# A third Strassen pair in the second w_o_b group, with memory statistics, value forms and one join moved

## The chip, the core and the metric

The kernel runs on one core of one Trainium2 chip. The metric is the device time of one launch in microseconds (us). The core's engines work side by side, each through its own list of instructions in order: PE (matrix products; PEld is its loading of the stationary operand), DVE (elementwise vector work), ACT (elementwise scalar work and copies), POOL, and SP, which here issues nearly all transfers. They wait for one another through semaphores.

## The reference

One layer of a streaming encoder for 256 tokens of width 2048, in float32. Cut to what matters:

```python
h = LN(alpha*h + 0.5*SwiGLU_1(h))                       # ffn1: 2048 -> 2*5504 -> 2048
proj = h @ w_in                                          # q/k/v of A, latents of B, both gates
y_a = chunked_relbias_attention(...) @ w_o_a
y_b = mla_attention(...) @ w_o_b                         # w_o_b: 2048 x 2048
h = LN(alpha*h + (g_a*y_a + g_b*y_b) @ w_out)            # w_out: 2048 x 2048
m = LN(mem)                                              # 256 memory tokens
q = h @ w_xq;  k, v = split(m @ w_xkv)                   # cross-attention, 4 heads of 512
h = LN(alpha*h + softmax(q k^T) v @ w_xo)
h = LN(alpha*h + 0.5*SwiGLU_2(h))                        # ffn2
```

## The kernel before, in words

**Numbers.** Every operand of a product is split in two: `hi`, a rounded copy that ACT makes (`halves` and `split`, lines 264 and 255), and `lo`, the rest, which DVE makes by a subtraction (lines 267 and 256). A product then takes three matmuls: hi by hi, hi by lo, lo by hi.

**Weights.** A weight arrives as 1 MB pieces (`raw`, a ring of three tiles) which SP loads, in the order of use. `load` in `run` makes `hi` and `lo` of a piece some pieces ahead of its use. An item of work with a weight is called a block here.

**Pairs of groups.** `pair_group` computes 1024 output columns (two times 512) for all 256 tokens in blocks that each cover two of the 16 tiles of 128 along the contraction. A plain block (`mm_pair`, line 311) is 2 tiles x 2 token halves x 2 column halves x 3 matmuls = 24 matmuls of 512 columns. A block that stands in the tuple `AT_...` is done as a Strassen pair (`mm_sums`, line 366): seven products in place of eight, so 21 matmuls. It costs more elsewhere. The seven products need sums of weights (`weight_sums`, lines 248 and 250 on DVE, into the tile that `sums_in` names), whose hi and lo are made as well, so that 3584 columns are split in place of 2048; and they need sums of activations, the forms (`forms_step`, `sum_forms`, lines 321 and 325, and a split). `SUMS_...` says where a form is kept: `None` is four small tiles of a ring, a name and a number is half of a block of memory that stays. At the end of the pairs `shared` (lines 679 to 684) combines the four shared sums out of PSUM.

**PSUM.** There are eight banks, four called `mm` and four called `at`. A group uses four for its own sums and the other four for its pairs' shared sums; the next group takes the banks over as they come free.

**Order.** `weave(main, side)` puts side work in front of the item with the given number of a group's list: numbers 0 to 7 are mostly the blocks, and `shared` takes a number of its own behind the last pair. A planner that knows costs then orders each engine's instructions; among work that is ready, what stands earlier in the program goes first, and a `prio` (SOON is 400 instructions) moves work ahead.

**The places that the change touches.**

- `out_b(g)`, group g of 0 and 1 of `w_o_b`. In group 0 the blocks 2, 4 and 6 are pairs, in group 1 the blocks 4 and 6. When a group ends, its `done` (lines 1282 to 1284) scales and adds with the gates, copies planes, and the sides `send` (a transposing transfer on SP) and `turn` (`join`, line 854 on ACT, then a split) prepare the input of `w_out`. The sides of group 0 run inside group 1, those of group 1 inside `w_out`.
- `mem_norm`, which normalizes the memory tokens beside the blocks of `w_out`: `stat(0)` and `stat(1)` take mean and spread of each half (four `bn_stats`, line 390, a chain of small DVE operations, two products with the identity, line 1358), `spread` broadcasts them with small matmuls (line 1368), and `quarter(0..3)` applies them. `stat` is bound to come behind the last `lo` before it, `spread` behind the last matmul before it.
- `cross`, whose `val(0)` computes half of the values in eight blocks of `w_xv` with pairs at 2, 4 and 6. `form_v(2)` is made in the group before, `form_v(4)` and `form_v(6)` inside `val(0)`, into block T3.
- `ffn`, whose last group of columns has 384 columns a side in place of 512 (n = 3). The hidden activations of the group before it are joined and split (`turn` in `hidden`) inside it. Each `ffn` has one such group.

Of the kernel before, what the change touches and what calls it, by code (L numbers as in the profile page):

```python
# [30 lines left out]
            {3: ("X1", 0), 5: ("X1", 1), 7: ("X0", 0)})  # L31
SUMS_GATE, AT_GATE = {**SUMS_IN, 5: ("F", 0)}, ((2, 4, 5, 6), (2, 4, 5, 6), (2, 4, 6), (2, 4, 6))
ORDER_GATE = (0, 2, 1, 4, 5, 3, 6, 7)
SUMS_YB = {4: ("T0", 0), 6: ("T0", 1), 2: None}
AT_YB = (2, 4, 6), (4, 6)
SUMS_XQ = {4: ("H5", 0), 6: ("H5", 1), 2: None}
SUMS_XV = {4: ("T3", 0), 6: ("T3", 1), 2: None}
SUMS_XO = {2: None, 4: ("H2", 0), 6: ("H2", 1)}
# [63 lines left out]
class Kernel:  # L102
# [451 lines left out]
    def ffn(self, tag, xT, st, first=None, steps=None, late=None, before=None, tags=None):  # L554
# [4 lines left out]
        turn = None  # L559
        fx = {}  # L560
        for half, nf in enumerate(F_SPLIT):
# [3 lines left out]
            for g in range(-(-nf // 4)):  # L565
                j, n = f0 // 4 + g, min(4, nf - 4 * g)
                qs, ps = {}, {}
                if j == 2 and first is not None:
                    self.add(self.load_rest)
                if j == 0 and first is not None:  # L570
                    main, (ps, qs, fx) = [], first
                    self.add(lambda qs=qs: self.shared(qs, 512), prio=SOON)
                elif j == 0 and before:
                    main = self.collect(self.first_group, tag, xT, before, ps, fx)
                else:
                    src = t[tag + "_w_in"][j] if n == 4 else t[tag + "_w_in_r"][0]
                    main = self.collect(self.pair_group, bank, src, n * P, KT, xT, SUMS_IN, fx, ps, qs, None, SUM_HOME + ("H5",))
                if turn and n < 4:
                    turn[5] = turn.pop(6)
                self.weave(main, turn or {}, prio=0)  # L580
                for c, (home, _) in homes.items():
                    if home == "X1" and c // 2 == g - 1:
                        self.add(form(c))
                hidden, turn = self.hidden(ps, bank, g, n, hid, qs)
                self.add(hidden, prio=SOON)
                if before and 2 <= j < 6:
                    self.add(lambda q=j - 2: self.gb_apply(2, self.h, (q,)), prio=LATE)
                if j == 0 and first is not None:
                    for c in set(SUMS_IN) - set(AT_FIRST):
                        self.add(self.forms_step(fx, SUMS_IN, c, xT, False))  # L590
                bank ^= 1
# [14 lines left out]
            side = dict(turn)  # L606
# [9 lines left out]
            turn = None  # L616
# [714 lines left out]
    def mem_norm(self):  # L1331
# [12 lines left out]
        def stat(tt):  # L1344
            def fn():
                if tt == 0:
                    e["diag"] = self.w2((P, 4, P))
                    e["ones"] = self.w1((P, P))
                    nc.gpsimd.memset(e["ones"], 1.0)
                st = self.ln_begin()  # L1350
                with self.tc.issue_after(self.last_lo.ins):
                    for n in range(4):
                        self.ln_piece(st, e["m"][tt], n)
                kept = self.chain
                mean, r, _ = self.ln_scale(st)
                self.chain = kept
                for k, v in enumerate((mean, r)):
                    nc.vector.tensor_scalar(e["diag"][:, 2 * k + tt, :], self.ident, v, None, ALU.mult)
                if tt:
                    e["mT"] = self.act(["H0", "H1", "H2", "H3"])  # L1360
            return fn
# [10 lines left out]
        def quarter(q):  # L1372
            def fn():
                v = e["raw"][q // 2][:, q % 2 * 4:q % 2 * 4 + 4, :]
                for k, op in enumerate((ALU.subtract, ALU.mult)):
                    nc.vector.tensor_tensor(v, v, e["mr"][:, k].to_broadcast([P, 4, S]), op)
                for j in range(4):
                    kt = 4 * q + j
                    nc.scalar.activation(v[:, j, :], v[:, j, :], AF.Identity,
                                         bias=self.vec("mem_ln_b", kt), scale=self.vec("mem_ln_g", kt))  # L1380
                self.split(v, e["mT"].blk(0, 4 * q, 4), e["mT"].blk(1, 4 * q, 4))
            return fn

        return {0: [load], 2: [stat(0)], 6: [stat(1)], 8: [spread], 9: [quarter(0)], 11: [quarter(1)], 13: [quarter(2)], 14: [quarter(3)]}

    def turned_norm(self, ln, st, x):

# [45 lines left out]
    def cross(self, xT, st, norm, steps_out):  # L1433
# [116 lines left out]
        form_v = lambda c: self.forms_step(fv, SUMS_XV, c, m)  # L1550
# [3 lines left out]
        def group(build, side, *args):  # L1554
            got = {}
            main = self.collect(lambda: got.update(build(*args) or {}))
            self.weave(main, side, prio=0)
            return got

        def both(one, two):  # L1560
            return {i: one.get(i, []) + two.get(i, []) for i in {*one, *two}}
# [9 lines left out]
                     8: [nsend(1, 3), njoin(1, 2)]}, 0, 8)  # L1571
        side = group(query, {1: [njoin(0, 3)], 2: [njoin(1, 3), form_q(4)], 4: [form_q(6)], 6: [form_q(2)]}, 0)
        side = group(query, both(side, {4: [form_v(2)]}), 1)
        group(val, both(side, {2: [form_v(4)], 4: [form_v(6)]}), 0)
        group(keys, {0: [ready(0)], 2: [scores(0), gb(0)], 3: [send(0), ready(1)], 4: [gb(1)], 5: [join(0), scores(1)],
                     6: [out(0), ready(2), send(1), gb(2)], 8: [join(1)]}, 8, KT)
        group(val, {1: [out(1), ready(3), scores(2)], 3: [send(2), scores(3), gb(3)], 5: [join(2), send(3)],
# [199 lines left out]
```

## Time and profile before

| what | us |
|---|---|
| median of 3 runs (lowest, highest) | 2434.77 (2434.17, 2435.91) |
| the profiled execution: its time | 2432.52 |
| the profiled execution: its span | 2430.7 |
| PE busy | 2422.3 |
| DVE busy | 2130.9 |
| ACT busy | 1553.2 |
| PE idle and waiting for another engine, all waits | 4.1 |

The profiled execution took 2.25 us less than the median. Its span runs from the first to the last instruction; 1.8 us of its time lie around it. Starts and stretches are given in us from the start of the span. In a row of the timeline, the number in brackets is the idle time of the engine before the row and what ended it; a row that stands for several instructions ends with their count, and the length of a row of matmuls includes 0.16 us of the last one's drain, in which the next has begun. In a row of windows there stand the length of the stretch, the busy time of each engine with the count of the instructions that touch the stretch, the granted TensorE clock (1.00 is full), the busy share of the DMA engines and GB/s.

The stages that the change touches, by the start of their first matmul:

| stage | us |
|---|---|
| last group of ffn1 | 547.90 to 580.81 |
| w_o_b, group 0 | 1200.94 to 1242.42 |
| w_o_b, group 1 | 1242.42 to 1284.58 |
| w_out, group 0 | 1284.58 to 1329.07 |
| first half of the keys | from 1373.50 |
| values, val(0) | 1502.22 to 1545.08 |
| last group of ffn2 | 2286.50 to 2319.49 |

### The profile page before, as it was taken

The numbers are of one execution on the slowest core, as the hardware profiler recorded it, in microseconds if no ns is written. First come the engines' busy times: TensorE is split into PE (matmuls) and PEld (weight loads), VectorE is DVE, ScalarE is ACT, GpSimd is POOL, SyncE is SP. The second block draws the span as 40 slices with busy tenths as digits, with TensorE's granted clock in tenths as the row PEclk, the third lists the DMA queues.
The fourth block names the chain that finished last, engine by engine and source line by source line (L and its number), as shares of the span: only waits on it lengthen the run. The fifth ranks groups of instructions, "written<-read, shape, count | busy, mean of one in ns | idle before, by whom it ended". The sixth has DMA issues, their size and how long they took to land.

```text
span 2430.7 us, 29702 instructions
## 1 busy us (share of the span) xinstructions
PE 2422.3 (100%) x11280; PEld 2022.8 (83%) x11280; DVE 2130.9 (88%) x2437; ACT 1553.2 (64%) x2022; POOL 35.9 (1%) x81
## 2 busy tenths in 40 slices
PE   9999999999999999999999999999999999999999
PEld 8888888888888888888888888888888888888887
DVE  8999989899889998779788889979879999888997
ACT  6676745666555557878565687765666675556662
POOL 0000000000000001000000000000000000000000
PEclk9999999999999999999999999999999999999999
DMA  7766656667656657776577577655556766666665
GB/s 268 252 212 214 207 200 222 210 201 219 224 176 215 216 195 248 229 210 176 183 246 256 167 241 213 220 181 192 190 199 214 229 221 210 220 207 207 200 220 182
DMA packets 176414, 516.20 MB, mean 212 GB/s; under 512 B 111728, under 2 KB 112496, under 8 KB 121104
## 3 DMA queue, kind: packets, MB, share of 16 engines
q1 hardware_dynamic: 170816, 495.83, 61.6%
q0 software_dynamic: 4592, 17.30, 2.2%
q8 instruction: 88, 1.44, 0.2%
q10 hardware_dynamic: 864, 1.18, 0.1%
q14 instruction: 54, 0.44, 0.1%
HBM read 485.30 MB, written 2.10 MB: 201 GB/s over the span
## 4 chain that ended last, share of the span: by engine, by line
PE 89%; DVE 4%; ACT 3%; DMA 1%; issue 1%; SPq 0%; DVEq 0%; ACTq 0%
PE at L311 24%; PE mm L311 23%; PE at L366 11%; PE mm L366 11%; PE mm L298 10%; PE mm L277 4%; PE mm L279 2%; DVE lo L267 2%; ACT hi L264 1%; PE at L1034 1%; PE at L1505 0%; PE at L277 0%; DMA raw<-w_xv 0%; PE at L1088 0%; ACT H L854 0%
## 5 line engine op out<-in xcount | busy, mean ns | idle before, releaser
L264 ACT CAST hi<-raw 128x1024 fp32r<-128x1024 f32 (+1 forms) x852 | 804.0, 981 | 458.0 <-PE at L311 150.1
L267 DVE TENSOR_TENSOR lo<-raw,hi 128x2048 fp32r<-128x2048 f32 (+1 forms) x427 | 902.0, 2114 | 134.8 <-ACT hi L264 129.0
L311 PE MATMUL mm<-hi,T 128*128 128x512 f32 (+1 forms) x1312 | 307.5, 384 | 0.8 <-DVE v L400 0.7
L311 PEld LDWEIGHTS mm<-hi,T 128*128 128x128 f32 x1312 | 244.5, 188 | 46.9 <-DVE v L400 1.1
L264 ACT CAST X<-H 128x1024 fp32r<-128x1024 f32 (+1 forms) x170 | 174.8, 1035 | 160.9 <-DVE H L248 119.9
L311 PE MATMUL at<-hi,T 128*128 128x512 f32 x1136 | 272.3, 390 | 0.0
L311 PEld LDWEIGHTS at<-hi,T 128*128 128x128 f32 x1136 | 213.3, 188 | 44.5
L267 DVE TENSOR_TENSOR X<-H,X 128x2048 fp32r<-128x2048 f32 (+1 forms) x85 | 191.4, 2252 | 64.7 <-ACT X L264 64.7
L311 PE MATMUL mm<-lo,T 128*128 128x512 f32 (+1 forms) x656 | 158.4, 383 | 0.0
L311 PE MATMUL at<-lo,T 128*128 128x512 f32 x568 | 141.0, 389 | 0.0
L311 PEld LDWEIGHTS mm<-lo,T 128*128 128x128 f32 x656 | 122.3, 188 | 22.4
L311 PE MATMUL at<-hi,H 128*128 128x512 f32 x560 | 133.8, 390 | 0.0
L311 PEld LDWEIGHTS at<-lo,T 128*128 128x128 f32 x568 | 106.7, 188 | 22.1
L311 PEld LDWEIGHTS at<-hi,H 128*128 128x128 f32 x560 | 105.0, 188 | 21.5
L250 DVE TENSOR_TENSOR H<-H,raw 128x512 f32<-128x512 f32 (+1 forms) x170 | 115.4, 679 | 2.2
L311 PE MATMUL mm<-hi,H 128*128 128x512 f32 x480 | 115.5, 392 | 0.1
L311 PEld LDWEIGHTS mm<-hi,H 128*128 128x128 f32 x480 | 89.6, 188 | 18.9 <-DVE w L684 0.5
L248 DVE TENSOR_TENSOR H<-raw 128x1024 f32<-128x1024 f32 (+1 forms) x85 | 102.1, 1201 | 0.6 <-DMA raw<-w_gate 0.4
L366 PE MATMUL mm<-X,X 128*128 128x512 f32 x342 | 91.4, 393 | 0.0
L264 ACT CAST X<-raw 128x1024 fp32r<-128x1024 f32 (+1 forms) x54 | 55.4, 1035 | 47.9 <-DVE raw L250 38.6
L366 PE MATMUL at<-X,X 128*128 128x512 f32 (+1 forms) x315 | 82.6, 386 | 0.7 <-ACT X L264 0.7
L854 ACT COPY w<-w 128x1024 uint16<-128x1024 uint16 (+1 forms) x60 | 75.7, 1275 | 1.4 <-DMA w<-w 1.4
(387 smaller groups left out, 4151.3 us busy)
## 6 DMA issues: line engine op xcount, KB each, us to landing
raw<-ffn_w_in SPq DMA_DIRECT2D x150, 1024.0 KB, 4.9
raw<-ffn_w_out SPq DMA_DIRECT2D x66, 1024.0 KB, 4.9
raw<-w_gate SPq DMA_DIRECT2D x32, 1024.0 KB, 4.8
raw<-ffn_w_out_r SPq DMA_DIRECT2D x16, 1024.0 KB, 4.9
raw<-w_qk SPq DMA_DIRECT2D x16, 1024.0 KB, 5.6
raw<-w_o_b SPq DMA_DIRECT2D x16, 1024.0 KB, 4.8
raw<-w_out SPq DMA_DIRECT2D x16, 1024.0 KB, 5.0
raw<-w_xk SPq DMA_DIRECT2D x16, 1024.0 KB, 5.4
```

Source lines behind the costliest of these rows:

```text
L248: self.nc.vector.tensor_tensor(two[0], two[1], raw[:, :m].unsqueeze(1).to_broadcast([P, 2, m]), ALU.add)
L250: self.nc.vector.tensor_tensor(t[:, a * m:a * m + m], t[:, b * m:b * m + m], raw[:, a * m:a * m + m], ALU.add)
L264: self.last_hi = self.nc.scalar.copy(hi[:, c:d], src[:, c:d])
L267: self.last_lo = self.nc.vector.tensor_tensor(lo[:, :n], src, hi[:, :n].bitcast(F32), ALU.subtract)
L277: self.nc.tensor.matmul(ps, hi[j], x.both(kt), start=(j == 0), stop=False)
L279: self.last_mm = self.nc.tensor.matmul(ps[:, :S], lo[j], x.at(0, kt), start=False, stop=(j == n - 1))
L298: self.last_mm = self.nc.tensor.matmul(ps, x.at(xi, kt)[:, tt * P:(tt + 1) * P], w[wi][:, j * 512 + c:j * 512 + c + m], start=(start and j ...
L311: self.last_mm = self.nc.tensor.matmul(ps[tt, g][:, :n], x.at(xi, kt)[:, tt * P:(tt + 1) * P], w[wi][:, c:c + n], start=first and j + wi + ...
L366: self.last_mm = self.nc.tensor.matmul(bank[:, :m], a[xi], v[wi][:, c * m:(c + 1) * m], start=own and first and wi + xi == 0, stop=own and ...
L854: self.nc.scalar.copy(self.words(u, n).rearrange("p (c k) -> p k c", k=2), self.words(s, n).rearrange("p (k c) -> p k c", k=2))
L1034: nc.tensor.matmul(ps[:, c0:c0 + nk], q[:, tt * P:(tt + 1) * P], k[:, :nk], start=(j == 0), stop=(j == len(parts) - 1))
```

## The change

Four things are changed.

1. `w_o_b`, group 1, takes block 2 as a pair as well, like group 0. The form of block 2, which both groups now use, moves from the four small tiles into block F, where the gates kept the form of their fourth pair. The host lays out the weights of that block accordingly; their bytes are the same.
2. In `mem_norm` the side numbers move: `stat(0)` from 2 to 4, `stat(1)` from 6 to 7, `spread` from 8 to 9, `quarter(0)` from 9 to 10.
3. In `val(0)` the forms move ahead: that of block 4 from 2 to 1, that of block 6 from 4 to 3.
4. In the last group of each `ffn` the `turn` of the group before moves from 5 to 7, that is from in front of block 5 to behind block 6, the last pair, just ahead of `shared`.

```diff
-SUMS_YB = {4: ("T0", 0), 6: ("T0", 1), 2: None}
-AT_YB = (2, 4, 6), (4, 6)
+SUMS_YB = {4: ("T0", 0), 6: ("T0", 1), 2: ("F", 0)}
+AT_YB = (2, 4, 6), (2, 4, 6)
...
                 if turn and n < 4:
-                    turn[5] = turn.pop(6)
+                    turn[7] = turn.pop(6)
...
-        return {0: [load], 2: [stat(0)], 6: [stat(1)], 8: [spread], 9: [quarter(0)], 11: [quarter(1)], 13: [quarter(2)], 14: [quarter(3)]}
+        return {0: [load], 4: [stat(0)], 7: [stat(1)], 9: [spread], 10: [quarter(0)], 11: [quarter(1)], 13: [quarter(2)], 14: [quarter(3)]}
...
-        group(val, both(side, {2: [form_v(4)], 4: [form_v(6)]}), 0)
+        group(val, both(side, {1: [form_v(4)], 3: [form_v(6)]}), 0)
```

## The prediction

> **What bounds the kernel.** I read the page first, then PE's waits, then PE's time block by block.
>
> ```profile
> span 2430.7 us, 29702 instructions
> ...
> PE 2422.3 (100%) x11280; PEld 2022.8 (83%) x11280; DVE 2130.9 (88%) x2437; ACT 1553.2 (64%) x2022; POOL 35.9 (1%) x81
> ```
>
> ```profile
> PE at L366 <- ACT X L264: 0.7, 2, 0.5
> PE mm L311 <- DVE v L400: 0.7, 1, 0.7
> PE mm L366 <- DVE T L256: 0.4, 1, 0.4
> ```
>
> PE stands still for 8.4 us of 2430.7. So only two things shorten this kernel: fewer matmuls, or taking away the few places where PE waits. But for one at the start these three are its longest waits, and they are where parts 2 to 4 of the change move something. The view rounds a wait to what is idle between two matmuls; what it costs shows better in the length of a block, from its first matmul to the next block's:
>
> ```profile
> core 0: us, PE busy (x), PEclk, DMA share, GB/s
> 1211.82:1216.58 4.76, 4.76 (x22) 1.00 0.55 176
> 1253.30:1258.74 5.44, 5.44 (x25) 1.00 1.14 342
> 1306.34:1312.75 6.41, 5.74 (x26) 1.00 0.89 316
> 1523.65:1528.71 5.06, 5.05 (x23) 1.00 0.84 340
> 1534.15:1539.64 5.49, 5.09 (x22) 1.00 0.57 191
> 547.90:580.81 32.91, 32.72 (x185) 1.00 0.70 210
> 2286.50:2319.49 32.99, 32.45 (x184) 1.00 0.66 209
> 2290.69:2294.85 4.16, 4.16 (x26) 1.00 0.83 196
> ```
>
> Row 1 is a pair in w_o_b (21 matmuls; neighbours that touch the stretch are counted too), row 2 the plain block that is to become one (24), both without a pause at full clock. Row 3 is block 4 of w_out, 0.97 us over a plain block's 5.44. Rows 4 and 5 are blocks 4 and 6 of val(0), 0.30 and 0.73 over a pair's 4.76. Rows 6 and 7 are the last groups of ffn1 and ffn2. Row 8, a plain block there, gives 4.16/24 = 0.1733 us a matmul; 5 plain blocks and 3 pairs, 183 matmuls, are 31.72, so the groups lose 1.19 and 1.27.
>
> **Part 1, the third pair.** PE saves 5.44 - 4.76 = 0.68 us. DVE pays for it, in the group where it can least:
>
> ```profile
> 1242.40:1284.60 42.20, 42.20 (x188) 34.95 (x187) 37.72 (x34) 30.54 (x35) 1.60 (x3) 1.00 0.83 276
> ```
>
> ```profile
> 1250.18 2.29 DVE L267 TENSOR_TENSOR lo<-raw,hi 128x2048 fp32r<-128x2048 f32 x1
> 1252.39 1.22 DVE L1284 TENSOR_TENSOR H<-H 128x1024 f32<-128x1024 f32 x1
> 1253.72 2.29 DVE L267 TENSOR_TENSOR lo<-raw,hi 128x2048 fp32r<-128x2048 f32 x1
> 1255.93 1.22 DVE L248 TENSOR_TENSOR X<-raw 128x1024 f32<-128x1024 f32 x1
> 1257.19 1.42 DVE L250 TENSOR_TENSOR X<-X,raw 128x512 f32<-128x512 f32 x2
> 1259.01 1.76 DVE L267 TENSOR_TENSOR lo<-raw,hi 128x1536 fp32r<-128x1536 f32 x1 [0.40 <-PE at L311]
> 1260.69 2.29 DVE L267 TENSOR_TENSOR X<-X,H 128x2048 fp32r<-128x2048 f32 x1
> 1265.85 1.23 DVE L248 TENSOR_TENSOR X<-raw 128x1024 f32<-128x1024 f32 x1 [2.88 <-DMA raw<-w_o_b]
> ```
>
> The rows from 1255.93 to 1260.69 are all that DVE does for the pair at block 4: three sums, lo of 1536 columns, lo of 2048, together 1.22 + 1.42 + 1.76 + 2.29 = 6.7. The plain block's lo, which goes, is 2.29. So DVE gets 4.4 us more; busy 37.7 of 42.2 becomes 42.1 of 41.5. Its idle time in the group (4.5 us, of it 2.88 ahead of the last row and 0.40) is filled to the brim and it comes out some 0.6 us late. Is that late enough to stop PE? Block 2's lo (first row) is done at 1252.4, and the plain block wants it with its lo by hi matmuls, 16 x 0.227 = 3.6 after 1253.30, at 1256.9: 4.5 us to spare. As a pair it wants its last lo after 17 of 21 matmuls, at 1257.2, and the work is done 4.4 later, at 1256.8, if the line 1284 row does not go first, and at 1258.0 if it does. So block 2 loses nothing or up to 0.8. The next tight place is w_out's block 1, whose lo runs late behind the group's closing work:
>
> ```profile
> 1290.26 2.29 DVE L267 TENSOR_TENSOR lo<-raw,hi 128x2048 fp32r<-128x2048 f32 x1
> ```
>
> ```profile
> 1293.65 1.98 PE L311 MATMUL mm<-lo,X 128*128 128x512 f32 x8
> ```
>
> It is ready at 1292.55 and used at 1293.65: 1.1 to spare, 0.4 when PE comes 0.68 earlier, against 0.6 of lateness: a loss of 0.2. I charge 0.4 for both together, nearer to nothing than to 0.8 + 0.9. Net 0.3 gained; ends: 0.68 gained, 1.0 lost.
>
> What else belongs to it: ACT casts 1536 columns more, and is busy 30.5 of 42.2: hidden. The loads are as many and as large. The form of block 2 becomes one split of 512 columns instead of four of 128, in an earlier stage, and block F has been free since the gates: nothing on the path. It is less work for ACT and DVE in that stage, so if PE did wait for it there, it would be a gain.
>
> **Part 2, the memory statistics.** Block 4 of w_out (row 3) is the first to read T0, the join of group 1's first half.
>
> ```profile
> 1302.65 2.47 DVE L390 BATCH_NORM_STATS2 bn<-T 128x6 f32<-128x512 f32 x4
> 1305.04 2.28 DVE L267 TENSOR_TENSOR lo<-raw,hi 128x2048 fp32r<-128x2048 f32 x1
> 1307.23 0.26 DVE L395 BATCH_NORM_AGGREGATE mv<-bn 128x2 f32<-128x24 f32 x1
> 1307.40 0.63 DVE L256 TENSOR_TENSOR T<-H,T 128x512 fp32r<-128x512 f32 x1
> ```
>
> ```profile
> 1303.43 0.61 ACT L255 CAST T<-H 128x512 fp32r<-128x512 f32 x1
> ```
>
> ACT had T0's first hi at 1304.04, but DVE ran the four bn_stats of stat(0), then a lo, and only at 1307.40 T0's lo; PE, at 1306.6, waited. With stat(0) two places later the 2.47 us are gone from this spot: T0's lo can run at 1304.1, and its second half behind the long lo near 1307.0, just about when PE wants it (eight matmuls minus a few after 1306.34). I take 0.85 of the 0.97; ends 0 and 0.97. The bn_stats then fall between blocks 4 and 6, where the page shows no wait of PE. For stat(1) one place later is one block, 5.4 us:
>
> ```profile
> 1327.89 0.28 DVE L1358 TENSOR_SCALAR w<-ident,y 128x128 f32<-128x128 f32 x1
> ```
>
> ```profile
> 1329.07 1.05 PE L1368 MATMUL at<-w,w 128*128 128x128 f32 x8
> ```
>
> Its last product ends at 1328.2, 0.9 ahead of the spread on PE. Now it ends near 1333.6, and PE arrives near 1327.5. I expect the planner, which sees this, to set the spread's matmuls inside block 8 or 9: no cost. If it doesn't, this is the third rival. The quarters behind it feed the keys at 1373.50, 40 us later.
>
> **Part 3, the value forms.** In rows 4 and 5 PE waits for the forms' lo (the third wait above: line 256, T).
>
> ```profile
> 1534.65 0.69 DVE L256 TENSOR_TENSOR T<-w,T 128x512 fp32r<-128x512 f32 x1
> ```
>
> The form of block 6 is ready at 1535.34, in the middle of row 5. Started a block earlier it is ready about 4.8 us sooner, as is that of block 4; T3, which they overwrite, is read by the query group until 1502.2, ahead of both. So 0.30 + 0.73 = 1.03 goes. The same DVE work now stands in front of blocks 2 and 3, whose lo has no wait in the view. I take 0.95; ends 0 and 1.03.
>
> **Part 4, the joins.** The wait `PE at L366 <- ACT X L264` occurs in the two last groups:
>
> ```profile
> 2303.43 1.37 ACT L854 COPY w<-w 128x1024 uint16<-128x1024 uint16 x1
> 2304.66 1.03 ACT L264 CAST X<-H 128x1024 fp32r<-128x1024 f32 x1
> ```
>
> The join (first row) holds ACT for 1.37 us, and the hi of the pair's weight sums comes behind it; PE waits for that hi. Moved behind block 6, the join and its split leave this spot; the 0.7 of the view, with some refilling of PE around it, goes: I take 1.1 of the 1.19 + 1.27. It lands just ahead of `shared`, which empties the banks that the next group needs:
>
> ```profile
> 2321.75 0.55 DVE L684 TENSOR_TENSOR w<-w,at 128x384 f32<-128x384 f32 x1
> ```
>
> ```profile
> 2322.71 1.07 PE L311 MATMUL at<-hi,H 128*128 128x512 f32 x4
> ```
>
> The last bank is free at 2322.3 and used at 2322.7. The join's two lo, 0.6 each, can come in between on DVE, and the combining needs small tiles that the join holds: up to 1.2 - 0.4 = 0.8 lost, twice. I charge 0.1 each. Net 0.9; ends: 1.1 gained, 1.6 - 1.1 = 0.5 lost.
>
> No moved step issues a transfer; SP's and POOL's queues keep their order.
>
> **The sum.** 0.3 + 0.85 + 0.95 + 0.9 = 3.0 us. The profiled execution goes from 2432.5 to 2429.5; the median stands 2.25 above it, so 2434.8 - 3.0 = **2431.8**. That is 0.12% faster. About 0.2%, 4.9 us, is what a measurement of this kernel can tell from no change, so I forecast no change by that bound: the whole of the good ends is 0.68 + 0.97 + 1.03 + 1.1 = 3.8.
>
> **The rivals.**
>
> *The pair costs more than it saves.* DVE's 4.4 us also hold raw tiles longer. A load waits for the lo that frees its tile:
>
> ```profile
> 1254.96 1.42 SPq L193 DMA_DIRECT2D raw<-w_o_b  x2
> 1256.42 9.27 SPq L850 DMA_TRANSPOSE H<-H  x2
> ```
>
> The second load of the first row, block 6's, went out when block 3's lo ended, at 1256.0, and DVE met it at 1265.85, having waited 2.88. Sent 4.4 later it lands near 1270.2, and block 5's lo, wanted by PE near 1271.9, is queued behind the sums of block 6 on DVE: 1.22 + 1.42 + 2.29 after 1270.2 is 1275.1, a stall of up to 3.2 us; time 2431.8 + 2.8 = 2434.6. For it: the 2.88 us show that DVE stood before this load. Against it: with 4.4 us of backlog DVE reaches these sums later, and then lo of block 5 may go first. [...]
>
> *The joins only move their wait*: 0.5 lost instead of 0.9 gained: 2433.2. For it: 0.4 us to spare at the banks. Against it: the casts that stand behind the join in its new place are mostly the next group's, wanted later.
>
> *The other side: the spread stops PE.* If its matmuls stay between blocks 7 and 8, PE waits from 1327.5 to 1333.6, 6.1 us: 2431.8 + 6.1 = 2437.9, slower than before by 0.13%. It decides from a wait of 3.0 us on. For it: before, the planner had them exactly there with 0.9 to spare. Against it: it orders by what it expects, and PE shows no such wait anywhere.
>
> *Changes that do nothing*: if the waits of parts 2 to 4 return in full at a neighbouring block, only part 1 is left: 2434.5.
>
> **How the numbers follow.** Forecast, within 1.5 us of 3.0: 0.57. Pair too dear: 0.13. Joins only move: 0.12. Nothing but part 1: 0.08. Spread: 0.07. The rest, 0.03, is gains beyond the good ends by a better order. The range from 2429.0 (a good end of 3.8 and 2 us for the spread of the runs and a new order) to 2435.2 takes all but the spread rival and part of the rest. Faster by over 0.2% needs 4.9 us, more than the good ends: the 0.03 of the rest and one in eight of the forecast's cases, by the 1.7 us between the lowest and the highest run: 0.10. Slower by over 0.2% needs the spread rival and the pair's together, about half of the former's 0.07: 0.04. Within: 0.86.
>
> **What would show it.** Right: block 2 of w_o_b's group 1 takes 4.8 us; block 4 of w_out 5.4 to 5.6; val(0)'s pairs all 4.8; the last groups of the ffn under 32.5; the waits at L311 and L366 are gone from PE's list. Wrong: a wait of PE on `lo`, `X` or `H` in w_o_b's group 1 or the first blocks of w_out, on `w` at L1368, or on L684 at the first out block of an ffn.

## The result, and the profile after

The changed kernel takes 2436.25 us (median of 15 runs, 2435.07 to 2451.16) against 2434.17 for the kernel before beside it (15 runs, 2432.18 to 2436.22): ratio 1.0016, 95% interval 1.0009 to 1.0023. It is slower, by 2 to 6 us, and the forecast of 2431.8 (2429.0 to 2435.2) is missed on the other side.

The profiled execution was the longest of the 15 and is read further below. A second set of runs of the same kernel (`e4_again`) was profiled in an execution of 2436.72; its page is the one to compare:

```profile
span 2434.9 us, 29699 instructions
...
PE 2424.0 (100%) x11277; PEld 2019.8 (83%) x11277; DVE 2133.9 (88%) x2438; ACT 1554.4 (64%) x2021; POOL 35.8 (1%) x81
```

Three matmuls fewer, as meant (11280 to 11277), and a longer span. PE's waits in the same execution (us in total, times, longest), from that list:

```profile
PE mm L366 <- DVE X L267: 0.8, 1, 0.8
PE mm L311 <- ACT T L255: 0.6, 1, 0.6
PE mm L311 <- DVE w L684: 0.6, 2, 0.4
```

The three waits that the prediction quoted are gone from it (L366 on X, L311 on v, L366 on T). These came instead. The first is a wait for the lo of a pair's weight sums, in the group that got the third pair. Windows of the same execution, one for each stretch of the argument:

```profile
1254.32:1259.32 5.00, 5.00 (x23) 3.86 (x21) 3.84 (x3) 4.70 (x6) 0.54 (x1) 1.00 1.14 321
...
1280.03:1286.56 6.53, 5.74 (x25) 4.43 (x24) 5.69 (x6) 5.93 (x8) 0.00 (x0) 1.00 0.73 274
1286.56:1292.47 5.91, 5.74 (x25) 4.43 (x24) 5.91 (x9) 2.00 (x3) 0.53 (x1) 1.00 0.54 180
1303.42:1309.60 6.18, 5.61 (x26) 4.32 (x24) 4.61 (x3) 5.49 (x7) 0.00 (x0) 1.00 1.14 289
1309.60:1315.43 5.83, 5.83 (x24) 4.53 (x25) 4.58 (x5) 5.81 (x7) 0.00 (x0) 1.00 0.91 347
1331.75:1376.78 45.03, 44.82 (x202) 36.78 (x200) 38.10 (x41) 27.99 (x38) 0.00 (x0) 1.00 0.52 185
...
1538.79:1543.85 5.06, 5.04 (x22) 3.86 (x21) 3.94 (x3) 4.46 (x5) 0.00 (x0) 1.00 0.60 206
547.78:580.22 32.44, 32.44 (x184) 31.48 (x183) 30.64 (x36) 22.24 (x31) 0.00 (x0) 1.00 0.75 235
2290.66:2323.18 32.52, 32.52 (x184) 31.52 (x183) 30.71 (x36) 22.26 (x31) 0.00 (x0) 1.00 0.71 235
```

Row 1 is block 2 of w_o_b's group 1, now a pair. It was 5.44 and is 5.00, not 4.76. Rows 2 to 4 are block 7 of that group and blocks 0 and 3 of w_out: plain blocks, each 5.44 before, now 1.09, 0.47 and 0.74 longer (the pause of the last is its end: block 4 waits there for T0's first hi, the `T L255` of the list). Row 5, block 4 of w_out, fell from 6.41 to 5.83; row 6, from the spread to the keys, grew from 44.43 to 45.03:

```profile
1329.07:1373.50 44.43, 44.43 (x202) 36.95 (x201) 36.58 (x29) 28.54 (x38) 0.00 (x0) 1.00 0.56 191
```

(This row is the kernel before.) Row 7, block 6 of val(0), fell from 5.49 to 5.06, and the last group of each ffn fell by 0.47 against the first profile of before. So the parts do move what they were to move. But the pair loses about 1.9 us where it was to gain 0.3: 0.44 saved against 1.09 + 0.47 + 0.74.

### The profile page after: what moved, and what is told of

It is laid out like the page before. It is cut to its first block, busy times and chain, and to the rows that moved or that the text cites. A ratio compares the mean times of both kernels' runs of the same rounds, so it can differ in the third digit from the quotient of the medians.

```text
span 2449.3 us, 29699 instructions
## 1 busy us (share of the span) xinstructions
PE 2425.7 (99%) x11277; PEld 2021.1 (83%) x11277; DVE 2134.9 (87%) x2438; ACT 1554.9 (63%) x2021; POOL 35.9 (1%) x81
## 4 chain that ended last, share of the span: by engine, by line
PE 88%; ACT 3%; DVE 3%; DMA 3%; issue 1%; SPq 1%; DVEq 0%; ACTq 0%
PE at L311 24%; PE mm L311 23%; PE at L366 11%; PE mm L366 11%; PE mm L298 10%; PE mm L277 4%; PE mm L279 2%; ACT hi L264 2%; DVE lo L267 1%; PE at L1034 1%; DMA raw<-w_o_b 1%; DMA raw<-w_xq 1%; PE at L1505 0%; SPq L850 0%; PE at L277 0%
## 5 line engine op out<-in xcount | busy, mean ns | idle before, releaser
L311 PE MATMUL mm<-hi,T 128*128 128x512 f32 (+1 forms) x1312 | 307.9, 383 | 1.3 <-ACT T L255 1.0
L311 PEld LDWEIGHTS mm<-hi,T 128*128 128x128 f32 x1312 | 244.0, 188 | 48.0 <-ACT T L255 1.4
L311 PE MATMUL at<-hi,T 128*128 128x512 f32 x1120 | 270.2, 391 | 0.0
L311 PEld LDWEIGHTS at<-hi,T 128*128 128x128 f32 x1120 | 211.2, 189 | 44.6
L311 PE MATMUL mm<-lo,T 128*128 128x512 f32 (+1 forms) x656 | 158.1, 382 | 0.0
L311 PEld LDWEIGHTS mm<-lo,T 128*128 128x128 f32 x656 | 122.2, 188 | 22.4
L311 PE MATMUL at<-lo,T 128*128 128x512 f32 x560 | 139.0, 389 | 0.0
L311 PE MATMUL at<-hi,H 128*128 128x512 f32 x560 | 133.6, 389 | 0.0
L311 PEld LDWEIGHTS at<-lo,T 128*128 128x128 f32 x560 | 105.1, 188 | 21.9
L311 PEld LDWEIGHTS at<-hi,H 128*128 128x128 f32 x560 | 104.9, 188 | 21.6
L311 PE MATMUL mm<-hi,H 128*128 128x512 f32 x480 | 115.5, 391 | 0.8 <-DVE w L684 0.4
L311 PEld LDWEIGHTS mm<-hi,H 128*128 128x128 f32 x480 | 89.6, 188 | 19.9 <-DVE w L684 0.8
L366 PE MATMUL mm<-X,X 128*128 128x512 f32 x342 | 91.3, 392 | 0.0
L366 PE MATMUL at<-X,X 128*128 128x512 f32 (+1 forms) x315 | 82.7, 386 | 0.1
```

What stands on the lines that cost most here:

```text
L311: self.last_mm = self.nc.tensor.matmul(ps[tt, g][:, :n], x.at(xi, kt)[:, tt * P:(tt + 1) * P], w[wi][:, c:c + n], start=first and j + wi + ...
L366: self.last_mm = self.nc.tensor.matmul(bank[:, :m], a[xi], v[wi][:, c * m:(c + 1) * m], start=own and first and wi + xi == 0, stop=own and ...
```

## The experiments

"Pair alone" is part 1 without the others. Blocks are cut by the count of their matmuls, 24 or 21, from the first to the next block's first; where PE's order interleaves two neighbours, a wait can fall to either.

### Which part costs

`e4_again` is the change, repeated.

> The changed kernel once more, to have an execution that is not the longest of its runs. Theory A (the pair: the third pair fills DVE and ACT in w_o_b's group 1, loads go out later, PE waits there): about 2436, w_o_b's group 1 1.5 to 3 us longer than the 41.5 it should take, nearly all of it in the blocks 2 to 6. Theory B (the moved statistics cost it): group 1 within 0.5 us of 41.5, and w_out 1 to 2 us longer than before's 88.9. Theory C (nothing but slow transfers in single executions): 2434 or less in most runs, and no stage longer than before by over 0.5 us.

Measured: 2436.72 (11 runs, 2433.84 to 2442.8) against 2433.89 of before; ratio 1.0013 (1.0004 to 1.0022). The slowdown repeats. In the profile group 1 takes 43.13 us, 1.6 over the 41.5: the size of theory A, but not its place, since most of it stands at block 7 and not in the blocks 2 to 6.

`e1_pair`, part 1 alone:

```diff
-SUMS_YB = {4: ("T0", 0), 6: ("T0", 1), 2: None}
-AT_YB = (2, 4, 6), (4, 6)
+SUMS_YB = {4: ("T0", 0), 6: ("T0", 1), 2: ("F", 0)}
+AT_YB = (2, 4, 6), (2, 4, 6)
```

> Part 1 alone (the third pair with its form in F). Theory A: 2 to 4 us slower than before, at 2436 to 2438, with single runs up to 15 us longer, since nothing else gives time back. Theory B: 0.3 to 0.7 us faster. Theory C: within 1 us of before, in most runs 0.7 faster.

Measured: 2439.58 (2435.89 to 2445.14), ratio 1.0025 (1.0016 to 1.0033): 4 to 8 us slower, more than the whole change and than theory A said. In its profiled execution (2436.95) the blocks read as in the change: block 2 of group 1 saves 0.44, block 7 loses 1.11, blocks 0 and 3 of w_out 0.47 and 0.80.

`e2_rest`, parts 2 to 4 without the pair:

> Parts 2 to 4 without the pair. Theory A: 1 to 2.5 us faster than before, at 2432 to 2433, with runs as close together as before's. Theory B: 1.5 to 2.5 us slower than before. Theory C: 2 to 3 us faster.

Measured: 2435.55 (2432.97 to 2438.65), ratio 1.0005 (0.9996 to 1.0014). Not the 2.7 us of gain that the prediction's terms for these parts add up to; a gain over 1 us is outside the interval. That is below what theories A and C said. It does not exclude the 1.5 to 2.5 us of loss of theory B; the blocks do, since w_out takes 88.6 us here and 88.9 before.

`e3_stats`, part 2 alone (the sides' numbers of the statistics, the spread and quarter 0 as in the change):

> Part 2 alone (memory statistics moved). By the prediction 0.85 us faster, block 4 of w_out at 5.4 to 5.6 us in place of 6.4. Theory A: 0 to 0.9 faster. Theory B: 1.5 to 2.5 us slower, with PE waiting at block 4 of w_out and around the spread.

Measured: 2433.57 (2432.45 to 2440.18), ratio 1.0000 (0.9991 to 1.0009). Its windows for block 4 of w_out and for the stretch from the spread:

```profile
1308.76:1314.20 5.44, 5.44 (x25) 4.50 (x24) 3.46 (x4) 4.96 (x6) 0.00 (x0) 1.00 0.83 328
1330.52:1375.53 45.01, 44.80 (x201) 36.78 (x200) 38.10 (x41) 28.00 (x38) 0.00 (x0) 1.00 0.52 185
```

Block 4 is a plain block without a pause: 0.97 gained, the good end. The second row gives 0.58 of it back. PE's timeline in the run of parts 2 to 4 shows how:

```profile
1328.17 0.38 PE L1368 MATMUL at<-w,w 128*128 128x128 f32 x2
...
1329.55 0.60 PE L1368 MATMUL at<-w,w 128*128 128x128 f32 x4
...
1336.62 0.38 PE L1368 MATMUL at<-w,w 128*128 128x128 f32 x2
...
1337.67 0.50 PE L311 MATMUL at<-hi,X 128*128 128x512 f32 x1 [0.21 <-ACT w L1370]
```

The spread's eight small matmuls, one run before, now stand in three pieces inside the blocks. Behind each piece the block's next matmuls take some 0.1 us more than their count at 0.227 (in the same timeline 1.41 us for 5, 1.86 for 7 and 0.71 for 2, each with 0.16 of drain), and after the last one a block waits 0.21 us for the bank that the spread used, until ACT has copied it.

So of the three theories the first comes nearest: the pair is the costly part, and "nothing but chance" is out. The time cannot place the moved statistics to better than 2 us either way; by the blocks they give 0.4 net.

### The parts one by one, and how far one profile repeats

`e0_before` is the kernel before, again.

> The kernel before, unchanged, for a second profiled execution of it on this chip. If the stage lengths of one kernel repeat, every block of the second w_o_b group and of w_out is within 0.1 us of the first profile; stages before the second w_o_b group may differ by up to 1 us in sum. What all variants showed alike against the first profile (block 0 of val(0) +0.35, keys and queries +0.1 to +1.1) is then seen here too, and belongs to the execution, not to the change. If instead it belongs to the edits, this profile repeats the first one there within 0.1 us.

Measured: 2433.87, one execution. w_o_b and w_out repeat the first profile within 0.1 us, block by block. Elsewhere it does not repeat; windows of block 4 of val(0) and of the last groups of the two ffn:

```profile
1524.51:1530.41 5.90, 5.05 (x23) 3.87 (x21) 5.54 (x5) 5.90 (x7) 0.00 (x0) 1.00 0.89 335
...
547.98:580.61 32.63, 32.45 (x184) 31.65 (x183) 30.33 (x35) 22.90 (x31) 0.00 (x0) 1.00 0.71 212
2288.20:2320.85 32.65, 32.40 (x184) 31.61 (x183) 30.36 (x35) 22.91 (x31) 0.00 (x0) 1.00 0.65 211
```

In the first profile they were 5.06, 32.91 and 32.99. The last groups were thus 0.3 us shorter with nothing changed, and block 4 of val(0) 0.8 longer.

`e5_forms`, part 3 alone (`{2: [form_v(4)], 4: [form_v(6)]}` becomes `{1: [form_v(4)], 3: [form_v(6)]}`):

> Part 3 alone (value forms a block earlier). The prediction: block 4 of val(0) falls from 5.06 to 4.8 and block 6 from 5.49 to 4.8, 0.95 us in all, nothing lost elsewhere. The rival, from the run of parts 2 to 4: block 6 falls by 0.4 only, to 5.1, because the lo of the pair's weight sums (X) is then the last to come, and block 4 does not fall; 0.4 us in all. The time cannot tell 0.4 from 0.95; the block lengths can.

Measured: 2433.71 (10 runs, 2432.76 to 2435.43), ratio 0.9997 (0.9988 to 1.0006). Block 6 of val(0):

```profile
1534.70:1539.79 5.09, 5.04 (x22) 3.86 (x21) 3.98 (x3) 4.46 (x5) 0.00 (x0) 1.00 0.63 208
```

0.40 gained, as in the change; block 4 was 5.24, within what it does by itself. The rival holds: 0.4, not 0.95.

`e6_joins`, part 4 alone (`turn[5]` becomes `turn[7]`):

> Part 4 alone (the join of the last group of each ffn behind block 6). The prediction: each last group 0.45 us shorter (32.90 to 32.45, 32.99 to 32.55), nothing lost behind them, 0.9 us in all. The rival, that the wait moves: the groups are shorter by the same, and the output stages behind them (103.62 and 111.25 us) are longer by about 0.4 us each, at the combining of the shared sums in front of the first output block; nothing gained in all.

Measured: 2433.58 (10 runs, 2432.69 to 2436.41), ratio 0.9999 (0.9990 to 1.0008). The last groups:

```profile
547.70:580.23 32.53, 32.53 (x184) 31.46 (x183) 30.67 (x36) 22.38 (x31) 0.00 (x0) 1.00 0.78 234
2288.16:2320.69 32.53, 32.53 (x184) 31.52 (x183) 30.60 (x36) 22.24 (x31) 0.00 (x0) 1.00 0.73 233
```

Against the second profile of before that is 0.10 and 0.12 gained, and the stage behind the second group took 111.32 where it was 111.26. The moved wait, the rival, is not there either. But a single profile is a poor measure of this part. In the sixteen profiled executions without it the group of ffn1 takes 32.57 to 32.90 and that of ffn2 32.65 to 33.59 (middle values 32.62 and 33.15); in the four with it, 32.29 to 32.53 and 32.39 to 32.60. By the middle values 0.2 and 0.6 are gained, though the time cannot show it. (In the change the stage behind the second group took 111.68. The matmuls in it are as before to 0.1 us; the 0.4 lies behind the last matmul, in the transfer of the output. It is there in each of the three profiles that hold parts 2 to 4 together, and its cause stays open.)

`e7_pair24` gives group 1 two pairs as before, at blocks 2 and 4, with the form in F:

```diff
-AT_YB = (2, 4, 6), (4, 6)
+AT_YB = (2, 4, 6), (2, 4)
```

> The second w_o_b group with two pairs, as before, but at blocks 2 and 4 in place of 4 and 6, and with the form of block 2 in block F as in the change. As many matmuls and as much weight-sum work as before. Theory A1 (three pairs are more work than DVE has room for between the group change and block 6): with two pairs there is room again, and the time is that of before, 2434 within 1.5 us; the blocks 6 and 7 and block 0 of w_out are not longer than before by more than 0.3 us. Rival A2 (a pair at block 2, next to the closing work of the first group, or its form in block F, is what costs): the loss of the pair alone stays, and the time is 2436 to 2440.

Measured: 2434.85 (2433.41 to 2437.05), ratio 1.0005 (0.9996 to 1.0014). The group, with as many matmuls as before, takes 0.47 us more: 0.26 in the 24 matmuls from block 2 on, 0.18 around block 4. From block 5 on and in w_out nothing is longer by more than 0.02. So the late losses do not come from the form in F, nor from a pair at block 2 by itself; an early loss of up to 0.5 does belong to a pair at block 2. This run has no pair at block 6, so it cannot tell whether it takes three pairs or only one at block 2 together with one at block 6.

### Is it DVE's room?

A weight block that is a pair asks this of DVE: line 248 and 250 sums from `raw`, the lo of three quarters, and the lo of the sums; ACT makes the hi of the sums (`H<-X`). Timelines of ACT and DVE before the change, at blocks 6 and 7:

```profile
1269.56 2.14 ACT L264 CAST H<-X 128x1024 fp32r<-128x1024 f32 x2
...
1275.07 1.99 ACT L264 CAST hi<-raw 128x1024 fp32r<-128x1024 f32 x2
```

```profile
1272.80 2.29 DVE L267 TENSOR_TENSOR X<-X,H 128x2048 fp32r<-128x2048 f32 x1
```

Both hi of block 6's sums come ahead of block 7's hi, and the sums' lo is done at 1275.1, some 4 us before block 7 starts. The same with the pair alone, SP first:

```profile
1255.51 5.20 SPq L193 DMA_DIRECT2D raw<-w_o_b  x2
```

```profile
1271.97 1.06 ACT L264 CAST H<-X 128x1024 fp32r<-128x1024 f32 x1 [1.35 <-DVE X L248]
1274.13 2.00 ACT L264 CAST hi<-raw 128x1024 fp32r<-128x1024 f32 x2 [1.10 <-DMA raw<-w_o_b]
1276.03 1.05 ACT L264 CAST H<-X 128x1024 fp32r<-128x1024 f32 x1
```

```profile
1255.86 2.29 DVE L267 TENSOR_TENSOR X<-X,H 128x2048 fp32r<-128x2048 f32 x1 [1.16 <-ACT H L264]
...
1264.58 2.29 DVE L267 TENSOR_TENSOR lo<-raw,hi 128x2048 fp32r<-128x2048 f32 x1
1266.79 2.28 DVE L267 TENSOR_TENSOR X<-X,H 128x2048 fp32r<-128x2048 f32 x1
1268.99 1.75 DVE L267 TENSOR_TENSOR lo<-raw,hi 128x1536 fp32r<-128x1536 f32 x1
1270.66 1.22 DVE L248 TENSOR_TENSOR X<-raw 128x1024 f32<-128x1024 f32 x1
...
1276.16 2.29 DVE L267 TENSOR_TENSOR lo<-raw,hi 128x2048 fp32r<-128x2048 f32 x1 [1.87 <-ACT hi L264]
1278.37 2.29 DVE L267 TENSOR_TENSOR X<-X,H 128x2048 fp32r<-128x2048 f32 x1
```

Block 6's load, the second of the SP row, goes out at its end, 1255.51 + 5.20 less the 0.33 of one issue, at 1260.38 instead of 1256.05 (so reckoned too), since DVE is late with the lo that frees its tile. It lands at 1265.8 all the same, as before: it takes 5.4 us in place of 9.7. Block 6's sums start at 1270.66 instead of 1265.85, 4.8 late, and what holds them is DVE's own list: from 1255.86 to 1274.28 DVE hardly pauses (18.29 us busy of 18.42), the 2.88 us of waiting are gone, and lo of block 5 and of block 6 (2.29 + 1.75), which ran behind these sums before, now stand ahead of them. Now the second hi of the sums stands behind block 7's hi on ACT, and that one waits for block 7's load (1.10). DVE has nothing that it may start, idles for 1.87, and the sums' lo is done at 1280.66 in place of 1275.09. PE wants it at 1279.9 and stands: the 0.8 of the list of waits, 1.1 in the block. The lateness goes on through the closing work, which starts at 1287.41 instead of 1284.93, to w_out. Over the whole group DVE is not full:

```profile
1242.66:1285.62 42.96, 38.93 (x35) 1.00 0.78 270
```

This row has DVE's busy time alone. Of the group's 42.96 us DVE idles 4.0, where it was 4.5 before. In place of the wait for a load there are three for ACT: 1.16 and 1.87 in the rows above, and 0.76 later on.

`e8_relief_pair` and `e9_relief` take 5.2 us of DVE's work out of the group's start, with and without the third pair:

```diff
-                        nc.vector.tensor_tensor(v[:, tt, 1, :], v[:, tt, 1, :], s, ALU.mult)
-                    nc.vector.tensor_tensor(v[:, :, 1, :], v[:, :, 1, :], v[:, :, 0, :], ALU.add)
+                        if g:
+                            nc.vector.tensor_tensor(v[:, tt, 1, :], v[:, tt, 1, :], s, ALU.mult)
+                    if g:
+                        nc.vector.tensor_tensor(v[:, :, 1, :], v[:, :, 1, :], v[:, :, 0, :], ALU.add)
```

> The third pair alone, with the closing work of the first group cut: its four multiplications by the gate (line 1283) and two additions (line 1284) are left out for group 0, so that the first half of B's output is not part of the result. That takes 4 x 0.68 + 2 x 1.22 = 5.2 us from DVE early in the second group, about what the third pair adds (4.4). To be read beside the next run, which leaves out the same and has no third pair. Theory A1 (DVE has no room for the third pair): now there is room; the load of block 6 goes out near 1256 as before the change, PE waits for no weight sums in the group, and this kernel takes 0.4 to 0.7 us less than the next one. Rival A2 (the loss of the pair comes from the transfers, their order or their collision, whatever DVE has to do): it still takes 2 to 5 us more than the next one.

> The kernel before with the same work left out in the closing work of group 0 (lines 1283 and 1284) and no third pair: the foil of the run ahead of it. Both theories: within 0.5 us of before, 2433.1 to 2434.1, since no wait of PE in the second group is there to be taken away.

Measured: 2433.02 (2431.54 to 2434.78) with the pair, ratio 0.9993 (0.9984 to 1.0001); 2434.36 (2432.52 to 2437.73) without, ratio 0.9997 (0.9989 to 1.0006). With room on DVE the pair is no longer slower; the difference of the medians, 1.3 us, is on the side of theory A1, though the intervals overlap. The blocks say it plainly. Windows of block 2 and block 7 of the group, and ACT's timeline, in the run with the pair:

```profile
1253.60:1258.36 4.76, 4.76 (x23) 3.94 (x22) 4.72 (x5) 2.67 (x4) 0.53 (x1) 1.00 1.02 319
...
1278.76:1284.19 5.43, 5.43 (x25) 4.50 (x24) 5.28 (x7) 2.15 (x4) 0.00 (x0) 1.00 0.68 249
```

```profile
1268.53 2.02 ACT L264 CAST H<-X 128x1024 fp32r<-128x1024 f32 x2
...
1273.90 2.02 ACT L264 CAST hi<-raw 128x1024 fp32r<-128x1024 f32 x2
```

The pair gives its full 0.68, nothing is lost behind it, and the hi of block 6's sums is back ahead of block 7's. Rival A2, transfers whatever DVE has to do, is out. That transfers have no part in it is not shown by this: with less to do on DVE they go out earlier too, and block 7's load takes 5.4 us here where it took 8.2 in the pair alone.

`e12_pair_pool_add` and `e13_pair_pool` leave nothing out and move the same work of group 0 from DVE to POOL: the additions, or additions and multiplications (`nc.vector` becomes `nc.vector if g else nc.gpsimd` on lines 1284 and 1283).

> The third pair alone, and the two additions of group 0's closing work (line 1284, 1.22 us each on DVE) done on POOL. Nothing is left out. Theory A1 (DVE has no room): 2.4 of the 4.4 us that the pair adds are given back, so the waits of PE in the group and in w_out (2.2 us in the pair alone) fall to about half or go: 2434 to 2436. Rival A2 (transfers, not DVE's room): they stay, 2437 to 2440.

> The third pair alone, and both the additions (line 1284) and the multiplications (line 1283) of group 0's closing work done on POOL: 5.2 us off DVE, nothing left out. Theory A1: no wait of PE in the group, block 2 at 4.76, and the time is 0.7 us under before, as with the work left out; between 2432.5 and 2434.5. Rival A3 (POOL is slower at it, 1.27 us for 512 columns in the one such row, so about 10 us in all, the transposes of group 0 go out later, SP's weight loads stand behind them, and PE waits for a load): 2435 or more, with waits on hi or on the turn's split.

Measured: 2437.22 (2435.52 to 2442.47), ratio 1.0016 (1.0007 to 1.0025); and 2440.8 (7 runs, 2440.26 to 2443.72), ratio 1.0030 (1.0020 to 1.0041). Both slower. By its time the first of them could be A2's; the blocks say that A3 decided, though by another queue than it named: block 7 and blocks 0 and 3 of w_out lose nothing now (under 0.1 us in the second kernel), but block 1 of the group is 2.1 and 6.0 us longer, block 4 of w_out 0.9 and 0.8, and in the first kernel block 1 of w_out 0.65. DVE, POOL and PE of `e13_pair_pool`:

```profile
1241.87 2.47 DVE L1282 TENSOR_TENSOR w<-w,mm 128x512 f32<-128x512 f32 x4
1244.26 3.07 DVE L267 TENSOR_TENSOR lo<-raw,hi 128x2048 fp32r<-128x2048 f32 x1
1247.25 4.59 DVE L250 TENSOR_TENSOR X<-X,raw 128x512 f32<-128x512 f32 x2
```

```profile
1245.26 4.32 POOL L1284 TENSOR_TENSOR H<-H 128x1024 f32<-128x1024 f32 x1
...
1253.06 2.34 POOL L1284 TENSOR_TENSOR H<-H 128x1024 f32<-128x1024 f32 x1
```

```profile
1258.94 1.22 PE L366 MATMUL at<-hi,T 128*128 128x512 f32 x2 [5.84 <-ACT hi L264]
```

The closing work's copies on ACT (line 846) wait 6.21 and 3.82 us for POOL, and block 2's hi stands behind them in ACT's queue. That the late losses are gone agrees with A1, but weakly, since PE comes by 2 to 7 us later and leaves DVE that time too. The cure is worse than the illness.

### The rest of the pair's loss

The profiled executions of the pair alone lose about 2 us by their blocks; its median loses 4 to 8. `e10_pair_hold` bound the four loads of the memory tokens behind the last matmul of w_o_b in the planner's order (`with self.tc.issue_after(self.last_mm.ins)` around the four `dma_start`).

> The third pair alone, with the four loads of the memory tokens (lines 1340 and 1342, 1 MB each) held until the last matmul of w_o_b, so that none of them runs beside the second group's transposes and its late weight loads. Theory T (the profiled loss of 2.2 us is DVE's, and what the median of the pair alone has beyond it, 5.7 less 2.2, is transfers of the second group slowed by the memory loads in a part of the executions): the median falls from 2439.6 to about 2436.5, and no execution is above 2441. Rival (the memory loads have no part in it): the median stays at 2438 to 2441 with the same spread of 9 us. A cost of the hold itself would show as waits of the statistics or the quarters in w_out.

Measured: 2439.01 (2435.41 to 2444.48), ratio 1.0016 (1.0007 to 1.0025). It says nothing on theory T: the loads still went out at 1253.35, 1264.08, 1274.11 and 1285.67. The order given to the planner did not hold them back here. What is left of it is a second sample of the pair alone.

`e14_pair_memT_late` made the two turned loads wait by data:

```diff
+                nc.vector.tensor_scalar(e["raw"][j][:, 0, :1], self.late(), 1.0, None, ALU.mult)
                 nc.gpsimd.dma_start(e["raw"][j], t["memT"][:, 8 * j:8 * j + 8, :])
```

> The third pair alone, with the two loads of the turned memory tokens (line 1342, 1 MB each) held by the data: DVE first writes one column of each tile from the end of the closing work of w_o_b's second group, so they go out near 1300 in place of 1265 and 1275. Two DVE instructions of about 0.1 us are added. Theory T (beyond DVE's 2.2 us, the pair's median loss is transfers of the second group slowed by the memory loads in part of the executions): the median falls from 2439.3 to about 2436.5, no execution above 2441. Rival: no part in it, 2438 to 2441 and the same spread.

Measured: 2438.34 (2436.54 to 2439.83), ratio 1.0018 (1.0009 to 1.0027). No execution is above 2440, where the pair alone has 5 of 11 and its second sample 4 of 11. Block 7 loses nothing, although block 6's sums start as late as in the pair alone (28.4 us after the group's first matmul; 28.0 there, 23.4 before): block 7's load takes 5.3 us in place of 8.2, ACT is not held up by it, and the sums' lo comes in time:

```profile
1276.64 2.28 DVE L267 TENSOR_TENSOR X<-X,H 128x2048 fp32r<-128x2048 f32 x1
```

So the loss at block 7 takes both, sums that are late on DVE and a load that lands later than ACT asks for it. But the hold costs 1.95 us at the spread (PE waits 1.7 there for the statistics' products on DVE) and 0.7 at block 4 of w_out beyond the pair alone, and the losses at blocks 0 and 3 of w_out stay (0.43 and 0.61), so the median falls by 1 us and not by 3. Half of theory T, then, and no proof.

`e16_pair_again` and `e17_pair_third` profiled the pair alone twice more.

> The third pair alone once more, for a second profiled execution. The waits in the second w_o_b group and in w_out are those of the first profile (2.2 us net, within 0.3) if they are in the program's order and not chance. About half of the pair's executions took 3 us or more beyond the first profiled one (2436.95). If this is such a one, theory T says that its extra time stands in the second w_o_b group, as late landings of weight loads beside transposes and memory loads; the rival says that it stands elsewhere or all over the kernel.

> The same again, for a third profiled execution of the pair alone; the same expectations as for the run ahead of it.

Measured: 2441.02 and 2437.48. The second repeats `e1_pair` block by block in w_o_b and w_out (block 7 by 1.11, blocks 0 and 3 by 0.43 and 0.95). The first is a long one, and its extra time stands in one place: block 6 of the group is 4.18 us longer than before instead of 0.02. ACT, PE and windows of it:

```profile
1273.19 1.05 ACT L264 CAST H<-X 128x1024 fp32r<-128x1024 f32 x1 [0.79 <-DVE X L248]
1278.47 1.99 ACT L264 CAST hi<-raw 128x1024 fp32r<-128x1024 f32 x2 [4.22 <-DMA raw<-w_o_b]
1280.36 1.04 ACT L264 CAST H<-X 128x1024 fp32r<-128x1024 f32 x1
```

```profile
1281.45 0.73 PE L366 MATMUL mm<-H,T 128*128 128x512 f32 x2 [2.87 <-ACT H L264]
```

```profile
1266.00:1270.00 4.00, 3.81 (x17) 2.81 (x17) 4.00 (x2) 3.55 (x5) 0.00 (x0) 1.00 1.43 114
...
1283.00:1285.00 2.00, 2.00 (x6) 1.51 (x6) 2.00 (x2) 2.00 (x4) 0.00 (x0) 0.50 1.05 418
```

It is the same order as above, with a later load: the second hi of block 6's sums stands behind block 7's hi, and that waits 4.22 us for its load. From 1266 to 1270, while the transposes and the first turned memory load run, the transfers moved 114 GB/s; in `e17_pair_third` the same window has 340. What SP had issued, the transposes for the most part, moved 0.42 MB in both; what POOL had issued, the memory load, moved 0.03 MB in place of 0.94. The first profile of the change, the one of 2451.16, is the same again, larger:

```profile
1287.72 1.99 ACT L264 CAST hi<-raw 128x1024 fp32r<-128x1024 f32 x2 [14.08 <-DMA raw<-w_o_b]
```

So what is lost beyond 2 us is, in the two long executions that were seen (one of the pair alone, one of the change), one late weight load; that the pair's median is long for the same reason is likely and not shown. Before the change block 7's load leaves at 1265.80, beside a transpose and the memory load as well, but block 6 does not stand behind it, and the few us until block 7 needs it are slack. Why the transfers are slow in some executions stays open, as does why the whole change has fewer long executions (above 2440: 3 of 15 and 1 of 11) than the pair alone.

### Candidates

`e11_stat0_forms`: the kernel before, `stat(0)` alone from 2 to 4, and part 3.

> A candidate: the kernel before with stat(0) alone moved from 2 to 4 (stat(1), spread and the quarters stay) and the value forms a block earlier; no third pair, joins as before. If the 0.6 us that the stretch with the spread lost in every run of the moved statistics comes from stat(1) and the spread having moved, block 4 of w_out is at 5.5 here and that stretch stays at 44.43: about 0.9 + 0.4 = 1.3 us faster than before, 2432.3. If it comes from stat(0), the stretch is at 45.0 and 0.7 is left.

Measured: 2434.67 (2431.43 to 2436.55), ratio 0.9996 (0.9987 to 1.0005). Block 4 of w_out is 5.47, the stretch of the spread 44.57, block 6 of val(0) 5.11: 0.94 + 0.38 gained, 0.14 lost. The cost at the spread came from moving stat(1) and the spread, not stat(0). The time cannot show 1.2 us.

`e15_best`: the pair with POOL's help, stat(0) and the forms.

> A candidate to beat both: the third pair with group 0's closing work (lines 1283 and 1284) on POOL, stat(0) alone moved from 2 to 4, the value forms a block earlier, joins as before. From the block lengths: 0.7 (pair) + 0.9 (block 4 of w_out) + 0.4 (block 6 of val(0)) = 2.0 us less than before, 2432; if A3 holds, not faster than 2434.

Measured: 2441.25 (6 runs, 2440.18 to 2443.02), ratio 1.0031 (1.0019 to 1.0043): A3 again. None of these kernels is measurably faster than the kernel before.

## Why the prediction was wrong

**Part 1** is where it failed. Its term was 0.3 gained, with 1.0 lost as the bad end; it lost about 1.9 in an undisturbed execution and 4 to 8 in the median.
- DVE's price was right: 4.4 us more (1.22 of it ahead of the group). The step that failed is that its idle time in the group "is filled to the brim and it comes out some 0.6 us late". It subtracted added work from idle time over the whole group. The 2.88 of idle time did go, but three waits for ACT came in its place, so DVE still idled 4.0 us of the group (4.5 before), and the added work came out as lateness: block 6's sums 4.8 us late and the closing work 2.5, not 0.6.
- "Block 2 loses nothing or up to 0.8": its last lo was foreseen at 1258.0 with line 1284 first and was done at 1258.15; PE took three matmuls of block 3 meanwhile, and 0.24 was lost.
- "The next tight place is w_out's block 1" was wrong. The tight place was block 6's own sums, in ACT's order, where the prediction had written "hidden". It counted ACT's busy time and not what stands behind what.
- The rival "the pair costs more than it saves" had half of the mechanism, an in-order queue. Its other half, block 6's load, did go out late (4.4 us foreseen, 4.3 measured), but landed at 1265.8 and not at 1270.2. It named the wrong queue and block (DVE, block 5) and stopped at 2434.6. It got 0.13 because "with 4.4 us of backlog DVE reaches these sums later, and then lo of block 5 may go first". That was true, and the stall moved to the next place.

**Part 2**: the term 0.85 was right for block 4 (0.97 alone, 0.58 in the change). The step "no cost" for the spread was wrong by 0.6, although its matmuls went inside the blocks as foreseen: split in three, they are not free. The rival "the spread stops PE" (6.1 us) did not happen.

**Part 3**: 0.95 was mis-sized. Block 6 gives 0.4; the rest waits for the pair's X (0.2 in the list of waits of `e5_forms`). Block 4's 0.30 was the first execution's: the same kernel had 1.14 over a pair in the second, and moving the forms does not shorten it.

**Part 4**: the term 0.9 came out at about 0.8 by the middle values of all profiles (0.2 and 0.6), and the wait on X is gone. That the size fits is in part luck: the prediction read it from one execution, and the second profile of before was 0.3 shorter in each group without the change.

**The sum**: by their blocks parts 2 to 4 give about 0.9 + 0.4 + 0.8, less 0.6 at the spread and 0.4 behind the last matmul, so 1.1 us and not 2.7, and nothing that their times can show. With part 1's loss the sum has the other sign. That the change stays within about 0.2% was foreseen and fits the ratio; the direction was not, and the range, which took "pair too dear" at 2434.6, ended 1 us short.

## What to carry to other kernels

DVE's idle time inside the group was not room that added work simply filled. One gap was filled (2.88 us) and others opened (1.16, 1.87 and 0.76; DVE's idle time in the group went from 4.5 us to 4.0), because DVE and ACT take turns: ACT's hi of the sums needs DVE's sums, the sums' lo needs that hi, and each engine went through its list in order (ACT stood 1.10 us for block 7's load, and in the long execution 4.22, with the second hi of the sums behind it). Before adding work, follow one late instruction along both lists: what now stands ahead of it, who waits for it, and what stands behind that one in the next list. And size a wait of under 1 us from two executions at least; here the same kernel's waits differed by 0.3 to 0.8 us where the blocks at the critical place repeated to 0.01.

## What the runs showed of the hardware

A pause of PE of 2.87 us cost more than itself: block 6 in `e16_pair_again` came out 4.18 us longer. The granted clock there is 0.80 from 1281 to 1283, 0.50 from 1283 to 1285, 0.84 from 1285 to 1287 and 1.00 from there to 1290.45, and the six matmuls from 1282.71 took 2.76 us, where six of the same kind from 1282.70 took 1.53 in `e4_again`. `e12_pair_pool_add`, with a pause of 1.9 us, has a mean clock of 1.0 over its execution, `e16_pair_again` 0.999.

At this work POOL was no spare DVE. In `e13_pair_pool` its two additions of 128 x 1024 took 4.32 and 2.34 us, where DVE takes 1.22; 2.34/1.22 = 1.92. Beside POOL's work DVE's lo took 3.07 instead of 2.29 and two sums 4.59 instead of 1.41, while the four rows at 1241.87, which read one operand from PSUM (`mm`), kept their pace (2.47 us for four; 1.28 for two before). The stretched rows read nothing from PSUM; that this is the cause was not shown.

Transposes and loads together moved 340 GB/s in one execution (`e17_pair_third`) and 114 in another of the same program (`e16_pair_again`), in the same stretch from 1266 to 1270 (the latter row is shown above). What SP had issued, the transposes for the most part, moved 0.42 MB in both; the memory load beside it moved 0.03 MB in place of 0.94. And a 1 MB load that SP issued 4.3 us later in `e1_pair` than before, just ahead of two transposes in both cases, landed at the same time (5.4 us in place of 9.7).
